# Where the sum of the four weight blocks of chunk 4 is made: by an adding transfer, or by VectorE

## The chip, the core and the metric

The kernel runs on one core of a Trainium2 chip. The metric is the device time of one execution in microseconds (us), as the median of several runs. The changed kernel is timed against the kernel before on the same chip.

The engines are TensorE (PE in the profile, its weight loads PEld), VectorE (DVE), ScalarE (ACT), GpSimd (POOL) and SyncE (SP). Each has its own list of instructions and works through it from the front. SP and POOL issue the transfers (DMA).

## The reference

Two layers of a hybrid model, on 256 tokens of width 1024, in float32. Each layer has two gated nets (`ffn1` and `ffn2`, with 2816 hidden columns), a mixer and a cross attention, each followed by a layer norm.

```python
def swiglu(x, w_gate, w_up, w_down):
    return (jax.nn.silu(x @ w_gate) * (x @ w_up)) @ w_down

for l in range(DEPTH):
    h = layer_norm(ALPHA * h + 0.5 * swiglu(h, ffn1_gate[l], ffn1_up[l], ffn1_down[l]), ...)
    ...  # mixer, cross attention
    h = layer_norm(ALPHA * h + 0.5 * swiglu(h, ffn2_gate[l], ffn2_up[l], ffn2_down[l]), ...)
```

The change lies in the first two products of a net, `x @ w_gate` and `x @ w_up`.

## The kernel before

**A product in three parts.** Each float32 operand is split into a rounded high part (ScalarE, line 75) and the low remainder (VectorE, line 76, which subtracts the high part that ScalarE has just made). TensorE multiplies high by high, high by low and low by high (line 132). So each raw weight tile of 128 x 1024 numbers (512 KB) that comes in costs a transfer, one cast on ScalarE (`whi`) and one subtraction on VectorE (`wlo`).

**A net.** The 2816 hidden columns are worked through in chunks: five of 512 columns and chunk 5 with 256. Between the products of a chunk, TensorE multiplies finished activations of earlier chunks with slabs of the `down` weights (`both`, `slab`; sums in the tiles `dn`). There are four nets. In the last three (`ffn2` of layer 0, `ffn1` and `ffn2` of layer 1) chunks 2, 3, 4 and 5 are made by `by_seven` (line 665).

**Seven products in place of eight.** For a chunk, gate and up weights are cut into an upper and a lower half of rows: `w00` is the gate's upper block, `w01` the up's upper, `w10` the gate's lower and `w11` the up's lower one. A block of a full chunk is two tiles of 128 x 1024. Two token tiles by two halves of x make a product of 2 x 2 by 2 x 2 blocks, and `by_seven` makes it with seven block products, from sums of weight blocks (built in place in `w00` and `w01`) and sums of x blocks (`bx`). The runs of a full chunk, in order:

1. `o` = x00 by `w00` (line 741); `w00 += w01` on VectorE, and `one` = bx0 by that (line 743).
2. `o` += x01 by `w10` (line 746).
3. `w00 += w11` on VectorE; `total` += bx1 by that (line 750). `less` is minus `total` (line 754).
4. `total` += bx2 by `w01` (line 757), which an adding transfer has made the sum of both up blocks.
5. VectorE reads `total` out (`put`, line 758, which runs line 721; it makes the tile `halves`).
6. `less` += bx3 by `w11` (line 759).
7. `total` += x11 by the sum of all four blocks (line 760). This adds to the bank that step 5 reads, so it can't start before step 5 is done.

The sum of all four blocks is made by `more(w00, gate, 1)` (line 752): POOL issues two transfers (line 738) that read the gate's lower block from memory once more and add it to `w00`, after the splits of `w00 + w01 + w11` have read it.

**Where the blocks lie.** The buffers of a chunk rotate (`homes`, lines 688 to 693). In chunk 4 of the three nets `w00` lies in two of the six `raw` buffers, `w01` in `spare0` and `spare1`, `w11` in `lng` and `lnb`, and `w10` in `spare2` and one `raw` buffer. Chunk 5 comes right behind and puts its own `w00` into `spare2`; its other three blocks and the `down` slabs take `raw` buffers. A load into a buffer waits until the last reader of what was there is done, and on SP all that is listed behind it waits with it.

**Order.** The engines' lists are made when the program is built, by a scheduler that looks at dependencies and priorities; a few places are tied by hand (`issue_after`). So an edit in one place can reorder its surroundings.

Of the kernel before, what the change touches and what calls it, by code (L numbers as in the profile page):

```python
# [28 lines left out]
CHUNK = 512  # L29
# [31 lines left out]
def model(ctx: ExitStack, tc: tile.TileContext, t: dict, out: bass.AP):  # L61
# [12 lines left out]
    def split(hi, lo, src):  # L74
        rounded = nc.scalar.copy(hi, src)  # L75
        lows.append(nc.vector.tensor_tensor(lo, src, hi.bitcast(F32), op=ALU.subtract))  # L76
        return rounded
# [78 lines left out]
    def mm_rows(o, xh, xl, wh, wl, start, stop, more=False):  # L156
        product(o, xh, wh, start, False, more)
        product(o, xh, wl, False, False, more)
        product(o, xl, wh, False, stop, more)

    def tok(i):
        return slice(i * P, (i + 1) * P)
# [313 lines left out]
    def ffn(l, name, n, pend=None, last=False, early=None, started=None, following=None):  # L476
        gate, up, down = (t[f"{name}_{x}"][l] for x in ("gate", "up", "down"))
        with tc.tile_pool(name="ffn", bufs=2, reuse_waits="tile") as fp:
# [186 lines left out]
            def by_seven(c0, ncol, bx, between):  # L665
                deep = 1024 // ncol

                def rows_by_columns(r):
                    return r.rearrange("p (k c) -> p k c", c=ncol)

                def pieces(*tags):
                    return [
                        rows_by_columns(
                            (fp if "spare" in g else wp).tile([P, DM], F32, tag=g, name="raw", bufs=6 if g == "raw" else 1)
                        )
                        for g in tags
                    ]
# [5 lines left out]
                def block(m, j, to):  # L683
                    for i, x in enumerate(to):
                        loads.append(nc.sync.dma_start(x, part_of(m, j, i)))
                    return to
# [7 lines left out]
                w00 = block(gate, 0, pieces(*homes[0]))  # L694
                w01 = block(up, 0, pieces(*homes[1]))
                w10 = block(gate, 1, pieces(*homes[3]))

                def parts_of(r, plus=None):
                    hi, lo = [], []
                    for i in range(len(r)):  # L700
                        if plus is not None:
                            nc.vector.tensor_tensor(r[i], r[i], plus[i], op=ALU.add)  # L702
                        h = wp.tile([P, 1024], F32R, tag="whi", name="whi", bufs=8)
                        w = wp.tile([P, 1024], F32R, tag="wlo", name="wlo", bufs=8)
                        h, w = (rows_by_columns(x) for x in (h, w))
                        split(h, w, r[i])
                        hi.append(h)
                        lo.append(w)
                    return Weights(hi, lo, deep, [])

                def part_of_x(i, j):
                    d = slice(4 * j, 4 * j + 4)
                    return xTh[:, d, tok(i)], xTl[:, d, tok(i)]

                def run(o, x, w, more=False):
                    for k in range(4):
                        wh, wl = w.at(k, slice(0, ncol))
                        mm_rows(o, x[0][:, k, :], x[1][:, k, :], wh, wl, k == 0 and not more, k == 3, more)

                def put(o, a, op, b):  # L720
                    nc.vector.tensor_tensor(ordered(o), ordered(a), in_order(b), op=op)  # L721
# [8 lines left out]
                def bank():  # L730
                    return acc((P, CHUNK))[:, 0:ncol]
# [4 lines left out]
                def more(to, m, j):  # L736
                    for i, x in enumerate(to):
                        nc.gpsimd.dma_start(x, part_of(m, j, i), accum_op=ALU.add)  # L738

                o, total, one = (bank() for _ in range(3))  # L740
# [7 lines left out]
                activate(s, 0, o)  # L748
                w11 = block(up, 1, pieces(*homes[2]))
                run(total, bx[1], parts_of(w00, w11), True)  # L750
                if ncol == CHUNK:
                    more(w00, gate, 1)
                less = bank()
                copied = nc.scalar.mul(less, total, -1.0)
# [1 line left out]
                if ncol == CHUNK:  # L756
                    run(total, bx[2], parts_of(w01), True)
                    put(f, e, ALU.subtract, total)
                    run(less, bx[3], parts_of(w11), True)
                    run(total, part_of_x(1, 1), parts_of(w00), True)  # L760
                else:
                    run(less, bx[3], parts_of(w11), True)
                    run(total, bx[2], parts_of(w01), True)
                    put(f, e, ALU.subtract, total)
                    with tc.issue_after(copied.ins):
                        w = parts_of(w00, w10)
                    between[2]()
                    run(total, part_of_x(1, 1), w, True)
# [48 lines left out]
            sevens = (2, 4) if early is not None else (2, 3, 4, 5)  # L817
# [27 lines left out]
            for c, (c0, ncol) in enumerate(chunks):  # L845
                if not c:
                    acts.append(first()())
                    ys = [[acc((P, 512), "dn") for _ in range(2)] for _ in range(NT)]
                elif c in sevens:
                    half = []  # L850

                    def deal_last():
                        acts[4] = acts[4]()

                    left = by_seven(
                        c0, ncol, bx,
                        [lambda: both(*todo.pop(0))] * 2 if ncol == CHUNK else
                        [lambda: (half.append(slab(3, 0)), both(3, 0, half[0], (0,))), deal_last, lambda: both(3, 0, half[0], (1,))],
                    )
                else:  # L860
                    acts.append(hidden(c0)() if ncol == CHUNK else last_hidden(c0, turn_memory))
# [595 lines left out]
```

## Time and profile before

| | us |
|---|---|
| median of three runs (lowest, highest) | 1076.18 (1074.79, 1076.83) |
| the profiled execution | 1078.4 |
| its span, first to last instruction | 1076.5 |
| TensorE busy (matmuls) | 1050.8 (98%) |
| VectorE busy | 956.7 (89%) |
| ScalarE busy | 680.4 (63%) |
| GpSimd busy | 110.0 (10%) |

The trace tells of the profiled execution alone, and every place in it is given in us from the start of its span. Rows of the timeline give the start, the time taken, engine, line, operation, output and inputs, the number of like instructions merged, and in brackets the idle time of the engine before it with what ended it. Operations of helpers all have the helper's line: line 76 is every low part, line 132 nearly every matmul.

### The profile page before, as it was taken

The page shows a single profiled execution, that of the slowest core. Times are in us where ns is not written, and L with a number is a line of the kernel's source. Part 1 is how long each engine was busy: PE and PEld are TensorE (multiplying, and loading weights), DVE is VectorE, ACT ScalarE, POOL GpSimd, SP SyncE. Part 2 cuts the span into 40 slices and gives each one's busy share as a digit, 9 for nine tenths or more (in the row PEclk, how much of TensorE's full clock was granted, in tenths as well). Part 3 has the DMA queues.
Part 4 walks back from the last instruction along what each step waited for, and adds up shares of the span by engine and source line. Part 5 has one row for each costly group of instructions (what it writes and reads, how often), then busy time and mean ns, then how long its engine had stood idle before and what let it go on. Part 6 is the DMA issues. An engine that isn't in the chain of part 4 may idle for free.

```text
span 1076.5 us, 16511 instructions
## 1 busy us (share of the span) xinstructions
PE 1050.8 (98%) x5978; PEld 930.9 (86%) x5978; DVE 956.7 (89%) x1257; ACT 680.4 (63%) x936; POOL 110.0 (10%) x140
## 2 busy tenths in 40 slices
PE   9999999999999999998999998999999999999987
PEld 7888888989899888887888887998998998888876
DVE  6998898989989789998998998899899779889988
ACT  6675775676466557666657566676773657557661
POOL 8001001000000001110001101010000000011101
PEclk9999999999999999999999998999999999999999
DMA  9999985854676589998789999766646665899972
GB/s 364 290 297 296 256 276 158 260 175 122 224 262 208 175 263 269 265 280 251 247 274 278 279 274 258 257 226 226 204 131 217 213 234 172 261 284 275 260 233 69
DMA packets 145569, 257.35 MB, mean 239 GB/s; under 512 B 11440, under 2 KB 52176, under 8 KB 145488
## 3 DMA queue, kind: packets, MB, share of 16 engines
q1 hardware_dynamic: 130656, 228.89, 63.9%
q0 software_dynamic: 14256, 26.23, 14.2%
q10 hardware_dynamic: 576, 1.18, 0.3%
q8 instruction: 47, 0.77, 0.3%
q14 instruction: 34, 0.28, 0.1%
HBM read 240.80 MB, written 1.05 MB: 225 GB/s over the span
## 4 chain that ended last, share of the span: by engine, by line
PE 70%; issue 12%; DMA 8%; DVE 7%; ACT 2%; POOL 1%; DVEq 0%; POOLq 0%; SPq 0%; ACTq 0%
PE acc L132 44%; PE dn L132 23%; DMA raw<-in_ffn_gate_dram 6%; DVE wlo L76 3%; ACT whi L75 2%; DMA raw<-in_ffn_up_dram 2%; DVE raw L702 1%; PE acc L199 1%; POOL raw L738 1%; DVE halves L721 0%; PE dn L1135 0%; DMA raw<-in_ffn_down_dram 0%; DVE h L407 0%; DMA h<-in_x_dram 0%; PE dn L1209 0%
## 5 line engine op out<-in xcount | busy, mean ns | idle before, releaser
L76 DVE TENSOR_TENSOR wlo<-raw,whi 128x1024 fp32r<-128x1024 f32 (+1 forms) x470 | 552.0, 1208 | 47.6 <-ACT whi L75 42.8
L75 ACT CAST whi<-raw 128x1024 fp32r<-128x1024 f32 (+1 forms) x470 | 471.1, 1041 | 187.5 <-DVE raw L702 75.2
L132 PE MATMUL acc<-whi,xT 128*128 128x512 f32 (+1 forms) x944 | 282.2, 376 | 13.8 <-DVE halves L721 13.5
L132 PEld LDWEIGHTS acc<-whi,xT 128*128 128x128 f32 x944 | 178.4, 191 | 39.9 <-issue 13.2
L132 PE MATMUL acc<-wlo,xT 128*128 128x512 f32 (+1 forms) x472 | 176.9, 375 | 0.2 <-DVE wlo L76 0.2
L132 PE MATMUL dn<-whi,ah 128*128 128x512 f32 x346 | 130.3, 381 | 2.2 <-ACT whi L75 2.2
L132 PE MATMUL dn<-wlo,ah 128*128 128x512 f32 x346 | 131.2, 379 | 0.0
L132 PE MATMUL dn<-whi,al 128*128 128x512 f32 x346 | 131.1, 379 | 0.0
L132 PE MATMUL acc<-xT,whi 128*128 128x512 f32 x480 | 117.6, 381 | 0.0
L132 PEld LDWEIGHTS acc<-wlo,xT 128*128 128x128 f32 x472 | 90.5, 192 | 12.6 <-DVE wlo L76 0.6
L132 PEld LDWEIGHTS acc<-xT,whi 128*128 128x128 f32 x480 | 86.8, 190 | 9.8
L132 PE MATMUL dn<-whi,xT 128*128 128x512 f32 x288 | 87.7, 380 | 0.0
L132 PE MATMUL acc<-whi,kTh 128*128 128x512 f32 (+1 forms) x224 | 80.2, 358 | 0.0
L132 PE MATMUL acc<-wlo,kTh 128*128 128x512 f32 (+1 forms) x224 | 79.9, 357 | 0.0
L132 PE MATMUL acc<-whi,kTl 128*128 128x512 f32 (+1 forms) x224 | 79.9, 357 | 0.0
L132 PEld LDWEIGHTS dn<-whi,ah 128*128 128x128 f32 x346 | 65.2, 189 | 12.1 <-ACT whi L75 3.4
L132 PEld LDWEIGHTS dn<-whi,al 128*128 128x128 f32 x346 | 65.4, 189 | 9.2
L132 PEld LDWEIGHTS dn<-wlo,ah 128*128 128x128 f32 x346 | 65.4, 189 | 9.1 <-DVE wlo L76 0.3
L132 PEld LDWEIGHTS acc<-xT,wlo 128*128 128x128 f32 x480 | 62.9, 191 | 3.2
L702 DVE TENSOR_TENSOR raw<-raw 128x1024 f32<-128x1024 f32 x53 | 63.8, 1216 | 0.2
L132 PE MATMUL acc<-xT,wlo 128*128 128x256 f32 x480 | 63.2, 275 | 0.0
L132 PEld LDWEIGHTS dn<-whi,xT 128*128 128x128 f32 x288 | 54.4, 189 | 7.5
(250 smaller groups left out, 1339.5 us busy)
## 6 DMA issues: line engine op xcount, KB each, us to landing
raw<-in_ffn_up_dram SPq DMA_DIRECT2D x88, 512.0 KB, 6.1
raw<-in_ffn_down_dram SPq DMA_DIRECT2D x88, 512.0 KB, 5.9
raw<-in_ffn_gate_dram SPq DMA_DIRECT2D x84, 512.0 KB, 6.0
raw<-in_w_in_dram SPq DMA_DIRECT2D x48, 512.0 KB, 4.7
raw<-in_ffn_up_dram POOLq DMA_DIRECT2D x25, 512.0 KB, 6.3
raw<-in_ffn_gate_dram POOLq DMA_DIRECT2D x22, 512.0 KB, 9.1
dealt<-sg SPq DMA_DIRECT2D x80, 128.0 KB, 4.6
raw<-in_ca_k_dram SPq DMA_DIRECT2D x16, 512.0 KB, 5.1
```

What stands on the lines that cost most here:

```text
L75: rounded = nc.scalar.copy(hi, src)
L76: lows.append(nc.vector.tensor_tensor(lo, src, hi.bitcast(F32), op=ALU.subtract))
L132: turns.append(nc.tensor.matmul(o, w, x, start=start, stop=stop, skip_group_check=more))
L199: turns.append(nc.tensor.transpose(pt[:, k, :], src[:, (4 * j + k) * P : (4 * j + k + 1) * P], unit))
L702: nc.vector.tensor_tensor(r[i], r[i], plus[i], op=ALU.add)
L738: nc.gpsimd.dma_start(x, part_of(m, j, i), accum_op=ALU.add)
```

## The change

In the last three nets, chunk 4 no longer issues `more(w00, gate, 1)`. Its step 7 passes `w10` to `parts_of`, which adds it to `w00` with two VectorE instructions (line 702) just before the splits. `w10` thus has to stay in its two buffers (`spare2` and one `raw`) until these are done. Chunks 2 and 3 of these nets and the first net are as before.

```diff
                 run(total, bx[1], parts_of(w00, w11), True)
-                if ncol == CHUNK:
+                by_transfer = ncol == CHUNK and (len(sevens) < 4 or c0 != 4 * CHUNK)
+                if by_transfer:
                     more(w00, gate, 1)
                 less = bank()
...
                     run(less, bx[3], parts_of(w11), True)
-                    run(total, part_of_x(1, 1), parts_of(w00), True)
+                    run(total, part_of_x(1, 1), parts_of(w00, None if by_transfer else w10), True)
                 else:
```

How the instructions move is shown for the first of the three nets; the other two move alike. First VectorE, at the end of chunk 4 and the start of chunk 5, before. Here `raw_4731` and `raw_4732` are the two tiles of chunk 4's `w00`, `raw_4851` and `raw_4852` those of its `w11`, `acc_4746` is `total`, `acc_4879` is `less`, and `raw_4980`, `raw_4982` and `raw_4984` are `w00`, `w01` and `w10` of chunk 5:

```order
L76 TENSOR_TENSOR wlo_4943<-raw_4852,whi_4942 128x1024
L76 TENSOR_TENSOR wlo_4959<-raw_4731,whi_4958 128x1024
L76 TENSOR_TENSOR wlo_4963<-raw_4732,whi_4962 128x1024
L76 TENSOR_TENSOR wlo_4991<-raw_4980,whi_4990 128x1024
L702 TENSOR_TENSOR raw_4980<-raw_4980,raw_4982 128x1024
L721 TENSOR_TENSOR halves_4744<-halves_4744,acc_4746 128x512
L76 TENSOR_TENSOR wlo_5009<-raw_4980,whi_5008 128x1024
L721 TENSOR_TENSOR halves_4744<-halves_4744,acc_4879 128x512
L76 TENSOR_TENSOR wlo_5027<-raw_4984,whi_5026 128x1024
```

And the same place with the change, where `raw_4739` and `raw_4740` are chunk 4's `w10`:

```order
L76 TENSOR_TENSOR wlo_4941<-raw_4852,whi_4940 128x1024
L702 TENSOR_TENSOR raw_4731<-raw_4731,raw_4739 128x1024
L702 TENSOR_TENSOR raw_4732<-raw_4732,raw_4740 128x1024
L76 TENSOR_TENSOR wlo_4958<-raw_4731,whi_4957 128x1024
L76 TENSOR_TENSOR wlo_4963<-raw_4732,whi_4962 128x1024
L721 TENSOR_TENSOR halves_4744<-halves_4744,acc_4746 128x512
L721 TENSOR_TENSOR halves_4744<-halves_4744,acc_4877 128x512
L76 TENSOR_TENSOR wlo_4991<-raw_4980,whi_4990 128x1024
L702 TENSOR_TENSOR raw_4980<-raw_4980,raw_4982 128x1024
L776 TENSOR_TENSOR sg_4743<-sg_4743,halves_4744 128x1024
L76 TENSOR_TENSOR wlo_5009<-raw_4980,whi_5008 128x1024
L76 TENSOR_TENSOR wlo_5027<-raw_4984,whi_5026 128x1024
```

The two sums of line 702 are new, both reads of chunk 4's results (line 721) stand ahead of chunk 5's first low part and first sum, where before they stood behind them, and the gating product (line 776, line 775 before) has come forward too.

Second SP, from the second tile of a `down` slab in chunk 4 on, before; `raw_4980`, `raw_4982`, `raw_4984` and `raw_5067` are the four blocks of chunk 5, one tile each:

```order
L98 DMA raw_4882<-in_ffn2_down_dram 128x1024
L685 DMA raw_4980<-in_ffn2_gate_dram 128x4x256
L685 DMA raw_4982<-in_ffn2_up_dram 128x4x256
L685 DMA raw_4984<-in_ffn2_gate_dram 128x4x256
L98 DMA raw_5042<-in_ffn2_down_dram 128x1024
L98 DMA raw_5043<-in_ffn2_down_dram 128x1024
L321 DMA lng_5156<-in_ln_g_dram 128x1024
L322 DMA lnb_5157<-in_ln_b_dram 128x1024
L685 DMA raw_5067<-in_ffn2_up_dram 128x4x256
```

And with the change:

```order
L98 DMA raw_4880<-in_ffn2_down_dram 128x1024
L685 DMA raw_4982<-in_ffn2_up_dram 128x4x256
L685 DMA raw_4984<-in_ffn2_gate_dram 128x4x256
L98 DMA raw_5042<-in_ffn2_down_dram 128x1024
L321 DMA lng_5156<-in_ln_g_dram 128x1024
L322 DMA lnb_5157<-in_ln_b_dram 128x1024
L685 DMA raw_4980<-in_ffn2_gate_dram 128x4x256
L98 DMA raw_5043<-in_ffn2_down_dram 128x1024
L685 DMA raw_5067<-in_ffn2_up_dram 128x4x256
```

Chunk 5's first block (`raw_4980`), whose buffer `spare2` now holds `w10` longer, has moved from ahead of its sister blocks to a place behind the two parameter rows of the layer norm.

On POOL the two adding transfers of each of the three nets are gone, six in all. ScalarE has as many instructions as before. TensorE has the same matmuls; between chunk 5's runs and the `down` products some have changed places.

## The prediction

> **What bounds the kernel now.** First the page's span and its row of TensorE, then the chain of waits of TensorE:
>
> ```profile
> span 1076.5 us, 16511 instructions
> PE 1050.8 (98%) x5978; PEld 930.9 (86%) x5978; DVE 956.7 (89%) x1257; ACT 680.4 (63%) x936; POOL 110.0 (10%) x140
> ...
> PE acc L132 <- DVE halves L721: 13.5, 4, 4.5
> ```
>
> TensorE is the bound: it sits idle for 25.7 us in all, and 13.5 of these in four waits for line 721, VectorE's read of a finished bank. The timeline of TensorE shows the three long ones, each in one of the three changed nets, at step 7 of chunk 4:
>
> ```profile
> 490.56 0.38 PE L132 MATMUL acc<-wlo,kTh 128*128 128x512 f32 x1
> 490.77 0.38 PE L132 MATMUL acc<-whi,kTl 128*128 128x512 f32 x1
> 494.71 0.45 PE L132 MATMUL acc<-whi,xT 128*128 128x512 f32 x1 [3.56 <-DVE halves L721]
> ...
> 660.03 0.38 PE L132 MATMUL acc<-whi,kTl 128*128 128x512 f32 x1
> 664.93 0.77 PE L132 MATMUL acc<-whi,xT 128*128 128x512 f32 x1 [4.52 <-DVE halves L721]
> ...
> 1024.91 0.38 PE L132 MATMUL acc<-whi,kTl 128*128 128x512 f32 x1
> 1029.30 0.76 PE L132 MATMUL acc<-whi,xT 128*128 128x512 f32 x1 [4.01 <-DVE halves L721]
> ```
>
> Matmuls follow each other at 0.21 to 0.22 us (490.56 to 490.77). From start to start, less 0.22, the stops cost 3.72, 4.68 and 4.17 us. The view by stretches shows that two of them cost more:
>
> ```profile
> core 0: us, PE busy (x) PEld busy (x) DVE busy (x) ACT busy (x) POOL busy (x), PEclk, DMA share, GB/s
> ...
> 494.70:497.50 2.80, 2.79 (x14) 2.48 (x15) 2.37 (x3) 2.80 (x4) 0.87 (x1) 1.00 0.55 104
> ...
> 664.90:670.20 5.30, 5.27 (x13) 4.21 (x14) 4.85 (x5) 3.26 (x4) 0.87 (x1) 0.50 0.70 100
> ...
> 1029.30:1032.40 3.10, 3.10 (x8) 2.49 (x9) 2.68 (x3) 3.10 (x4) 1.29 (x1) 0.51 0.25 32
> ```
>
> Behind the stops of 4.68 and 4.17 us the granted clock (PEclk) is 0.50 and 0.51, behind that of 3.72 it stays 1.00. Half of 5.3 us and half of 3.1 us are lost besides: 2.65 and 1.5. So this place loses 3.7, 7.3 and 5.7 us. The Trainium skill's page "TensorE: Matmul & The Clock Gate" (Part 1: The HAM clock gate) says that an idle window of about 3.4 us, which runs freely, halves the clock. The trace agrees: the two stops above 4 us did it, the one of 3.72 did not.
>
> What VectorE did meanwhile, in the first of the three nets (its timeline):
>
> ```profile
> 482.70 5.76 DVE L76 TENSOR_TENSOR wlo<-raw,whi 128x1024 fp32r<-128x1024 f32 x5
> 490.35 2.36 DVE L76 TENSOR_TENSOR wlo<-raw,whi 128x1024 fp32r<-128x1024 f32 x2 [1.89 <-ACT whi L75]
> 492.74 1.23 DVE L702 TENSOR_TENSOR raw<-raw 128x1024 f32<-128x1024 f32 x1
> 493.89 0.68 DVE L721 TENSOR_TENSOR halves<-halves,acc 128x512 f32<-128x512 f32 x1
> 495.13 1.22 DVE L76 TENSOR_TENSOR wlo<-raw,whi 128x1024 fp32r<-128x1024 f32 x1 [0.57 <-ACT whi L75]
> ...
> 500.28 1.22 DVE L702 TENSOR_TENSOR raw<-raw 128x1024 f32<-128x1024 f32 x1
> 501.42 1.22 DVE L775 TENSOR_TENSOR sg<-sg,halves 128x1024 f32<-128x1024 f32 x1
> ...
> 508.41 2.36 DVE L76 TENSOR_TENSOR wlo<-raw,whi 128x1024 fp32r<-128x1024 f32 x2 [1.11 <-ACT whi L75]
> ...
> 524.63 0.68 DVE L377 SCALAR_TENSOR_TENSOR h<-h,dn 128x512 f32<-128x512 f32 x1
> ```
>
> And what it waited for at 490.35: POOL's two adding transfers, the least, median and largest time from their issue to landing, and ScalarE's casts.
>
> ```profile
> 477.36 2.42 POOL L738 DMA_DIRECT2D raw<-in_ffn_gate_dram  x2 [10.19 <-DVE wlo L76]
> ...
> DMA to landing us min/median/max: 6.3/8.5/10.8
> ...
> 489.27 2.00 ACT L75 CAST whi<-raw 128x1024 fp32r<-128x1024 f32 x2 [3.05 <-DMA raw<-in_ffn_gate_dram]
> ```
>
> The second adding transfer landed 10.8 us after its issue at 478.5, at 489.3. The cast of its tile ended at 490.3 and the low part at 491.6. Line 721, which TensorE needs, stood behind that, one more low part and a sum: 493.89. Otherwise VectorE hardly rests: from 482.70 to 508.41 its idle time is 1.89, 0.57 and 1.11 us, 3.57 together. The x5 row gives its pace: five in 5.76 us, the last taking 1.22, so 1.14 from start to start.
>
> **The change, part by part**, in the times of the first net.
>
> *Removed:* two adding transfers of 512 KB and the wait for them. Their issue cost POOL alone.
>
> *Added:* two sums of 1.14 us on VectorE. Their inputs have long been there. They take the place of the last of the five low parts, at 487.25 and 488.39, and end at 488.47 and 489.6. The casts follow, each 1.04 long and some 0.1 behind its sum: 489.6 and 490.7. The low parts start at 489.65 and 490.8. Then line 721 comes at once: 491.9 to 492.6, and TensorE goes on 0.14 later, as it did before (494.57, 494.71): at 492.75 in place of 494.71. A stop of 1.75 us stays, too short for the low clock by the rows above.
>
> *Moved:* chunk 5's first block. SP's rows before, and then times to landing:
>
> ```profile
> 472.42 0.43 SPq L685 DMA_DIRECT2D raw<-in_ffn_gate_dram  x1
> ...
> 486.22 0.33 SPq L321 DMA_DIRECT2D lng<-in_ln_g_dram  x1
> 487.36 0.33 SPq L322 DMA_DIRECT2D lnb<-in_ln_b_dram  x1
> 488.49 0.38 SPq L685 DMA_DIRECT2D raw<-in_ffn_up_dram  x1
> ...
> DMA to landing us min/median/max: 5.9/5.9/5.9
> ...
> DMA to landing us min/median/max: 6.2/6.2/6.2
> ...
> DMA to landing us min/median/max: 5.8/5.8/5.8
> ...
> DMA to landing us min/median/max: 5.1/5.1/5.1
> ...
> 661.82 0.33 SPq L98 DMA_DIRECT2D raw<-in_ffn_down_dram  x1
> ...
> DMA to landing us min/median/max: 3.1/3.1/3.1
> ```
>
> The first landing is that of the row at 472.42, the block in question, which so lay there from 478.4 on. With the change its load waits for the first of the two sums and goes out at 488.5, just where the row at 488.49 stood. That row's landing is the second, and its like in the other two nets are the third and fourth: 6.2, 5.8 and 5.1 us, with adding transfers still on the way. The last, 3.1, is that of the row at 661.82, a tile of a `down` slab that went out alone. Queued on SP behind the new wait are another slab tile, which waits for the second sum, and chunk 5's last block: out at about 490.9 in place of 488.49, so landed by 497.1 even at 6.2, and VectorE adds it only at 500.28 or later. How long the moved load takes without the adding transfers no row shows: between 3.1 and 6.2. I take 4.6, the middle: landed at 493.1.
>
> From there a chain that was hidden before: cast 493.2 to 494.25; low part 494.3, for which VectorE has waited since 493.1; sum with `w01` 495.4 to 496.6; cast of it, behind an activation, 496.7 to 497.75; its low part 497.8, against 495.13 before. TensorE has finished step 7 at 495.35 (12 matmuls from 492.75), the first run of chunk 5 at 496.9, and waits for these: 0.2 at 495.4, 1.05 at 496.9, and about 1.05 more for the cast and low part behind it.
>
> On VectorE, up to the row of 508.41: work, plus 2 x 1.14 = 2.28. Idle: 1.2 for the block, 1.2 for the cast of chunk 5's next sum, since the gating product (at 501.42 before) that used to fill this gap now comes earlier, and 1.1 as before at the last sum: 3.5 against 3.57. So that row comes 2.1 to 2.2 us later. From there to the layer norm (524.63, which started without a wait) VectorE has no slack, and TensorE runs within half a us of it (it kept VectorE waiting 0.50 at 525.8):
>
> ```profile
> 525.82 0.69 DVE L377 SCALAR_TENSOR_TENSOR h<-h,dn 128x512 f32<-128x512 f32 x1 [0.50 <-PE dn L132]
> ...
> 511.25 0.35 PE L132 MATMUL acc<-whi,xT 128*128 128x256 f32 x1 [0.35 <-ACT whi L75]
> ```
>
> TensorE so arrives some 0.3 us less late: 1.8 later than before in this net. It had lost 3.7 there, and 0.5 at 511.25. So the same course with the change loses 4.2 + 1.8 = 6.0, now in many small stops.
>
> *The sum.* The other two nets have the same instructions there, so 6.0 each. Before, they lost 7.3 and 5.7. Differences: +1.8, -1.3, +0.3: +0.8 us on the profiled span of 1076.5. The span lies 1.9 below its execution's 1078.4, and the median of the runs is 1076.18; I carry the difference over to the median. Forecast: 1076.18 + 0.8 = 1077.0. About 0.2%, or 2.15 us, is what a measurement of this kernel can tell from no change.
>
> Bounds: each us by which the block lands later than 4.6 costs 1 us in each net: at 6.2, 3 x 1.6 = 4.8 more, 1081.8. Earlier helps little: the sum's cast stands behind the activation of step 7's result (TensorE's end 495.5, activation to 496.2), so at 3.1 only 0.4 per net, 1075.8. The Trainium skill's page "DMA: Bandwidth & Descriptors" (Anatomy of one DMA) fits 2.0 us plus bytes over 436 GB/s to a transfer on GpSimd's path, an estimate of 3.2 us for 512 KB. By it the sum would be 1075.8. The trace doesn't bear it out at this place, where GpSimd's two took 6.3 and 10.8; only the lone slab's 3.1 is as short.
>
> **The rivals.**
>
> *Slower: the moved load is late.* If it takes what its neighbours took, VectorE stands idle from 493.1 to as late as 495.8 and the clean stop of before is paid again in chunk 5. It decides from a landing of about 5.1 us on (0.8 + 3 x 0.45 makes the 2.15 of a measurable loss). For it: all three rows at that place. Against: these had the adding transfers beside them. Price 1081.8; 30%.
>
> *Slower: the low clock.* TensorE's work between 491 and 500 falls into pieces with some 4.5 us of stops. If that halves the clock as in two nets before, another 1.5 to 2.65 us go per net: 1081.5 to 1085.0. Against it: the longest piece is 1.75 us, and 3.72 passed unpunished. 9%.
>
> *Faster: VectorE has room after all.* If the three idle times (3.5 us a net) take up the two sums, so that no work is added in effect, the row of 508.41 comes 2.28 - 3.5 = 1.2 us earlier, and each net gains 2.1 + 1.2 = 3.3 against the forecast: 1077.0 - 9.9 = 1067.1. For it: the stops of before, 17 us in all, are the largest idle time in the kernel, and line 721 does come sooner. Against: the idle times are waits for casts of sums, which more speed elsewhere doesn't shorten. 20%.
>
> That the change doesn't do what it says is ruled out: the lists show six transfers gone and six sums added.
>
> **How the numbers follow.** Forecast 41%, late load 30%, faster 20%, low clock 9%. The forecast's own range is 1075.8 to 1081.8, and one row misread by 0.5 us a net moves it by 1.5. The whole range leaves out the lower half of the faster case and the upper part of the low clock: 1070 to 1083. Faster by over 0.2% (below 1074.0): the rival, and little of the forecast, 0.22. Slower (above 1078.3): both slower rivals, 0.39. Within: 0.39.
>
> **What would show it.** Right: the waits of TensorE for line 721 fall from about 3.6, 4.5 and 4.0 us to under 2 each; the granted clock stays near 1.00 behind them; the load of chunk 5's first block goes out right behind the rows of the layer norm and lands 4 to 5 us later; chunk 5 shows new stops of about 1 us. Wrong: no new stops in chunk 5 (the faster case), a landing of over 5.1 us, or a clock of 0.5 in chunk 5.

## The result, and the profile after

The changed kernel takes 1082.02 us (median of five runs, 1080.45 to 1083.80), the kernel before 1076.83 beside it (five runs, 1074.79 to 1078.40). The ratio is 1.0048, with a 95% interval of 1.0030 to 1.0066: slower by some 5.2 us, in the range of the prediction and above its forecast of 1077.0. Ratios here and below are of fast runs alone: of the six runs of e12, a kernel below, one took 1376.37 us at a granted clock of 0.752, which is left out of its ratio but not of its median of 1070.85 (1070.22 without it).

The profiled execution is the fastest of the five, 1080.45. The page's first lines and TensorE's waits:

```profile
span 1078.7 us, 16498 instructions
PE 1052.4 (98%) x5978; PEld 928.1 (86%) x5978; DVE 963.5 (89%) x1263; ACT 680.6 (63%) x936; POOL 102.7 (10%) x134
...
PE acc L132 <- DVE halves L721: 5.0, 3, 1.7
PE acc L132 <- ACT whi L75: 2.9, 4, 0.8
PE acc L132 <- DVE wlo L76: 2.8, 4, 0.9
PE acc L132 <- ACT acc L742: 2.5, 3, 0.8
```

VectorE has six instructions and 6.8 us more (six sums of 1.14). The waits for line 721 went from 13.5 to 5.0 us, three of at most 1.7. Waits of 0.8 to 0.9 us, of kinds that the kernel before had once each at most, have come in their place. In the first of the three nets TensorE's timeline has them in a row:

```profile
489.98 0.38 PE L132 MATMUL acc<-whi,kTl 128*128 128x512 f32 x1
491.94 0.45 PE L132 MATMUL acc<-whi,xT 128*128 128x512 f32 x1 [1.57 <-DVE halves L721]
...
496.37 0.38 PE L132 MATMUL acc<-wlo,xT 128*128 128x256 f32 x1 [0.88 <-DVE wlo L76]
498.70 0.38 PE L132 MATMUL acc<-whi,kTh 128*128 128x256 f32 x1 [0.84 <-ACT whi L75]
499.92 0.38 PE L132 MATMUL acc<-whi,xT 128*128 128x256 f32 x1 [0.84 <-ACT acc L742]
```

The first row stood at 490.77 before, so this execution comes to the place 0.79 us earlier; times below are often moved by such a shift, to the clock of the kernel before. The second row is step 7, and the matmuls of 256 columns are chunk 5. Row by row, TensorE's lateness against the kernel before grows by 3.4 us over this net (from -0.79 to +2.58 at 530.79), by 0.4 over the second and by 1.7 over the third, 5.4 together. Elsewhere the instructions are the same and the two executions still differ: the kernel before had a stop of 1.56 us at 964 that the changed one hadn't.

VectorE's timeline at the same place, with the sum at 509.03 being the third of chunk 5:

```profile
486.48 2.36 DVE L702 TENSOR_TENSOR raw<-raw 128x1024 f32<-128x1024 f32 x2
488.82 2.37 DVE L76 TENSOR_TENSOR wlo<-raw,whi 128x1024 fp32r<-128x1024 f32 x2
491.11 1.47 DVE L721 TENSOR_TENSOR halves<-halves,acc 128x512 f32<-128x512 f32 x2
495.09 1.23 DVE L76 TENSOR_TENSOR wlo<-raw,whi 128x1024 fp32r<-128x1024 f32 x1 [2.51 <-ACT whi L75]
496.35 1.22 DVE L702 TENSOR_TENSOR raw<-raw 128x1024 f32<-128x1024 f32 x1
497.49 1.22 DVE L776 TENSOR_TENSOR sg<-sg,halves 128x1024 f32<-128x1024 f32 x1
498.68 4.63 DVE L76 TENSOR_TENSOR wlo<-raw,whi 128x1024 fp32r<-128x1024 f32 x4
...
505.62 3.50 DVE L76 TENSOR_TENSOR wlo<-raw,whi 128x1024 fp32r<-128x1024 f32 x3 [1.17 <-ACT whi L75]
509.03 1.22 DVE L702 TENSOR_TENSOR raw<-raw 128x1024 f32<-128x1024 f32 x1
511.36 1.23 DVE L76 TENSOR_TENSOR wlo<-raw,whi 128x1024 fp32r<-128x1024 f32 x1 [1.11 <-ACT whi L75]
```

The largest idle time is 2.51 us, for the cast of chunk 5's first block. ScalarE's row says what that cast waited for, SP's rows when the load went out, and the view by source how long it took in the three nets:

```profile
494.01 1.04 ACT L75 CAST whi<-raw 128x1024 fp32r<-128x1024 f32 x1 [4.08 <-DMA raw<-in_ffn_gate_dram]
...
486.60 0.33 SPq L322 DMA_DIRECT2D lnb<-in_ln_b_dram  x1
487.74 0.38 SPq L685 DMA_DIRECT2D raw<-in_ffn_gate_dram  x1
...
DMA to landing us min/median/max: 6.2/6.2/6.2
...
DMA to landing us min/median/max: 5.5/5.5/5.5
...
DMA to landing us min/median/max: 5.7/5.7/5.7
```

It landed at 493.94. The granted clock (the third number from the end of a row), by stretches of the second net:

```profile
670.00:672.50 2.50, 0.89 (x4) 0.70 (x5) 2.50 (x3) 2.50 (x4) 1.29 (x1) 0.95 0.08 10
672.50:675.00 2.50, 2.50 (x14) 2.50 (x13) 2.50 (x3) 1.61 (x3) 0.00 (x0) 0.50 1.03 165
675.00:677.50 2.50, 2.50 (x16) 2.37 (x16) 1.51 (x2) 1.13 (x3) 0.00 (x0) 0.87 1.23 253
```

Behind chunk 5's cluster of short stops the clock was halved here. In the other two nets it stayed at 1.00.

### The profile page after: what moved, and what is told of

The parts are those of the page before. It is cut to its first block, busy times and chain, and to the rows that moved or that the text cites. A ratio compares the mean times of both kernels' runs of the same rounds, so it can differ in the third digit from the quotient of the medians.

```text
span 1078.7 us, 16498 instructions
## 1 busy us (share of the span) xinstructions
PE 1052.4 (98%) x5978; PEld 928.1 (86%) x5978; DVE 963.5 (89%) x1263; ACT 680.6 (63%) x936; POOL 102.7 (10%) x134
## 3 DMA queue, kind: packets, MB, share of 16 engines
q0 software_dynamic: 12624, 23.09, 12.5%
q10 hardware_dynamic: 576, 1.18, 0.3%
## 4 chain that ended last, share of the span: by engine, by line
PE 80%; DVE 8%; DMA 5%; ACT 4%; issue 3%; POOL 0%; DVEq 0%; ACTq 0%; SPq 0%
PE acc L132 54%; PE dn L132 23%; DVE wlo L76 5%; ACT whi L75 3%; DMA raw<-in_ffn_gate_dram 3%; DVE raw L702 1%; DMA dealt<-both 1%; PE acc L199 1%; DMA raw<-in_ffn_down_dram 1%; DVE square L531 1%; PE dn L1136 0%; DMA h<-in_x_dram 0%; PE dn L1210 0%; DVE al L76 0%; PE acc L581 0%
## 5 line engine op out<-in xcount | busy, mean ns | idle before, releaser
L702 DVE TENSOR_TENSOR raw<-raw 128x1024 f32<-128x1024 f32 x59 | 71.0, 1220 | 0.2
L738 POOL DMA_DIRECT2D raw<-in_ffn_up_dram x25 | 30.3, 1211 | 338.7 <-DMA raw<-in_ffn_down_dram 137.9
```

## The experiments

The first theory (T): the late load of chunk 5's first block is the loss. Its rival R1: the six sums are, by their time on VectorE. All ratios are against the kernel before on the same chip. The last two columns are of the first of the three nets: how much later than before chunk 5's third sum starts on VectorE (shifts at entry taken off), and what TensorE loses over the net. Before, the third sum is this row:

```profile
506.08 1.22 DVE L702 TENSOR_TENSOR raw<-raw 128x1024 f32<-128x1024 f32 x1
```

| kernel | median us | ratio (95%) | third sum | net |
|---|---|---|---|---|
| e3, no sums, load early | 1066.01 | 0.9910 (0.9897–0.9923) | -1.9 | -1.9 |
| e12, half the change, edge | 1070.85 | 0.9930 (0.9905–0.9954) | 0.0 | -0.3 |
| e5, before, edge | 1073.43 | 0.9967 (0.9953–0.9980) | 0.0 | -0.3 |
| e7, change, spare1, edge | 1074.23 | 0.9973 (0.9960–0.9985) | +1.0 | +1.2 |
| e6, change, edge | 1074.58 | 0.9983 (0.9970–0.9996) | +1.0 | +1.2 |
| e11, half the change | 1077.48 | 0.9993 (0.9977–1.0008) | +2.0 | +1.6 |
| e9, before, two edges | 1075.56 | 0.9998 (0.9983–1.0013) | +1.1 | +0.7 |
| e1, change, spare1 | 1078.15 | 1.0016 (1.0003–1.0030) | +2.0 | +1.7 |
| e2, change, sums early | 1078.60 | 1.0023 (1.0008–1.0037) | +1.3 | +1.6 |
| e8, change, rows behind | 1080.40 | 1.0040 (1.0024–1.0056) | +3.0 | +2.7 |
| e4, no sums, load late | 1080.08 | 1.0043 (1.0029–1.0057) | +1.9 | +2.1 |
| the change | 1082.02 | 1.0048 (1.0030–1.0066) | +3.7 | +3.4 |

One more kernel, e10, with both edges of e9 and the first of them at every full chunk, took 1106.51 us. It no longer computes the reference's result, so its time says nothing for or against a theory.

**e1, the load early, the sums kept.**

```diff
-                    homes = [("spare2",), ("raw",), ("raw",), ("raw",)]
+                    homes = [("spare1",), ("raw",), ("raw",), ("raw",)]
```

> The changed kernel with one word changed: in the last three nets, chunk 5's first block lies in spare1, which chunk 4's second block leaves free about 3 us earlier, not in spare2, which the two VectorE sums now hold to 487.7. The sums stay. Theory T (the loss is the late load of chunk 5's first block, landed 5.5 to 6.2 us after an issue that the sums hold back): the load goes out ahead of the layer-norm rows, 2 to 3 us earlier, VectorE's idle 2.51 us ahead of chunk 5's first low part is gone, TensorE's stops in chunk 5 fall from 4.4, 3.5 and 4.2 us to under 2 each, and the time is 1074 to 1078, 4 to 8 below the changed kernel's 1082.0. Rival R1 (the loss is the six sums themselves, 6 x 1.14 = 6.8 us of VectorE time): no change, 1080.5 to 1083.5. Rival R3 (the loss is the queue: whatever is moved, something of the layer-norm rows, the slab and the block is late): also 1080.5 to 1083.5, but with the stops at another place.

VectorE, chunk 5's first low part, first and third sum:

```profile
493.27 1.22 DVE L76 TENSOR_TENSOR wlo<-raw,whi 128x1024 fp32r<-128x1024 f32 x1
...
495.01 1.22 DVE L702 TENSOR_TENSOR raw<-raw 128x1024 f32<-128x1024 f32 x1
497.40 1.23 DVE L76 TENSOR_TENSOR wlo<-raw,whi 128x1024 fp32r<-128x1024 f32 x1 [1.18 <-ACT whi L75]
...
508.88 1.22 DVE L702 TENSOR_TENSOR raw<-raw 128x1024 f32<-128x1024 f32 x1
```

The load went out at 485.90 and landed at 489.58; the 2.51 us before the first low part are gone, and of the 5.2 us some 3.5 came back. T's range ends at 1078, the median is 1078.15: most of the loss goes with the late load, but 1.7 us stay that T has no place for. The edit moved more than the load: the gating product, which filled the wait behind the first sum in the changed kernel (497.49), stands behind the next low part here, and VectorE waits 1.18 us.

**e2, the sums early.** The two sums stand where the transfers were issued.

```diff
+                elif ncol == CHUNK:
+                    for y, z in zip(w00, w10):
+                        nc.vector.tensor_tensor(y, y, z, op=ALU.add)
```

> The changed kernel with its two VectorE sums made right after step 4's parts, where the kernel before issued the adding transfer, and not ahead of step 7's parts. The fourth block's tiles come free some 6 us earlier and chunk 5's first load goes out ahead of the layer-norm rows. The number of sums is the same. Theory T: chunk 5 starts with its block landed, no stop of over 0.3 us in its first rows, 4 us per net less lost there at most; 1072 to 1078. Rival R1 (the sums' VectorE time): VectorE does the same work ahead of step 7, so 1080 to 1083. A miss for both if the sums, put ahead of the parts of steps 5 and 6, make those late: then new stops at chunk 4's steps 5 and 6 of up to 2.3 us each, 1080 to 1086.

The third case of the expectation came, in another form. TensorE's waits and VectorE's row:

```profile
PE dn L132 <- DVE wlo L76: 7.4, 3, 2.5
...
482.82 9.16 DVE L76 TENSOR_TENSOR wlo<-raw,whi 128x1024 fp32r<-128x1024 f32 x8
```

The sums push the low parts of a `down` slab back, and TensorE stops up to 2.5 us for these in each net. The load is early here too (landed by 486.56), and some 2.7 of the 5.2 us came back: 1078.60 lies between the ranges, just above T's 1078 and under R1's 1080.

**e3 and e4, without the sums: load early, load late.** e3 leaves the fourth block's part of the sum out, and e4 all of it but two columns, whose sums hold `w10` as long as the change does. Shown against the changed kernel:

```diff
-  parts_of(w00, None if by_transfer else w10)
+  parts_of(w00)
+  # e4, ahead of it:
+  for y, z in zip(w00, w10) if not by_transfer else ():
+      nc.vector.tensor_tensor(y[:, 0, 0:2], y[:, 0, 0:2], z[:, 0, 0:2], op=ALU.add)
```

> The changed kernel without the two sums, and without the adding transfer: in the last three nets' chunk 4, step 7 multiplies by the sum of three weight blocks, the fourth block's part of it is left out. Nothing holds spare2, so chunk 5's first load goes out as early as in the kernel before. Theory T and rival R1 agree here: step 7's stop falls under 1 us (VectorE is done with w00's low parts 2.3 us earlier than in the changed kernel) and chunk 5 starts on time; the kernel before lost 4.2, 7.3 and 5.7 us at this place, so 1076.8 - 17.2 + 3 x (0.5 to 1.5) = 1061 to 1064, up to 1067. It is the floor against which the next kernel is read.

> As the kernel without the sums, but in their place VectorE adds two columns of the fourth block's tiles to the first's (128x2 in place of 128x1024): the fourth block is held as long as in the changed kernel, while VectorE does 2 x 1.1 us less. All but two columns of the fourth block's part of the sum are left out. It parts the two costs. Theory T (late load): chunk 5's block lands as late as in the changed kernel, its first parts wait for it, and most of the loss stays: 1074 to 1081, at least 8 us above the kernel without sums. Rival R1 (the sums' own time): the loss goes with the sums, 1061 to 1068, within 3 us of the kernel without sums.

VectorE in e3, chunk 5's first sum, and in e4, its first low part and first sum:

```profile
489.84 1.22 DVE L702 TENSOR_TENSOR raw<-raw 128x1024 f32<-128x1024 f32 x1
```

```profile
494.57 1.23 DVE L76 TENSOR_TENSOR wlo<-raw,whi 128x1024 fp32r<-128x1024 f32 x1 [2.56 <-ACT whi L75]
495.83 1.23 DVE L702 TENSOR_TENSOR raw<-raw 128x1024 f32<-128x1024 f32 x1
```

e3 comes out in its range, although step 7's stop stays at 1.8 to 1.9 us and doesn't fall under 1 (line 721 stands behind chunk 5's first sum there); e4 comes out 14 us above it, as T had it. But e1 is 12 us above e3 too, with the load early and only the sums added, which T can't explain. So each of the two alone takes 12 to 14 us of e3's gain, and both together 16. T as the only cause falls, and so does R1.

Neither edit is pure. Of e4's idle time 2.56 us is for the load, but 1.04 is for the cast behind its two short sums; in e1 1.18 is for the cast behind chunk 5's first sum. Up to the row behind the third sum VectorE is idle for 1.68 us in e3, 3.46 in e1, 5.28 in e4 and 4.79 in the changed kernel. With 2.28 us of sums in e1 and in the change, and some 0.2 in e4, that is 4.1, 3.8 and 5.4 us more than in e3; the third sum starts 3.9, 3.8 and 5.7 later. So the costs overlap because work of the one fills idle time of the other: in the changed kernel the second full sum fills the wait that e4 has behind its short ones, and the product fills the wait of e1.

I call what replaces T and R1 S: what counts is when VectorE gets through chunk 5's sums, by work and idle time together. The table's last columns bear it out: over all twelve kernels the net's cost on TensorE follows the third sum to within 0.5 us in the first net. In the second and third nets of the same traces it does so to within 0.7.

**e5, e6, e7: one order edge.** Line 721 for step 5 goes ahead of the low parts of step 7, in the kernel before (e5), the changed one (e6) and e1 (e7). In e6 and e7 the sums stand ahead of line 721.

```diff
-                    put(f, e, ALU.subtract, total)
+                    taken_out = put(f, e, ALU.subtract, total)
                     run(less, bx[3], parts_of(w11), True)
-                    run(total, part_of_x(1, 1), parts_of(w00), True)
+                    with ExitStack() as behind_put:
+                        if len(sevens) == 4 and c0 == 4 * CHUNK:
+                            behind_put.enter_context(tc.issue_after(taken_out.ins))
+                        w = parts_of(w00)
+                    run(total, part_of_x(1, 1), w, True)
```

> The kernel before, with its adding transfer, and one order edge: in the last three nets' chunk 4, VectorE takes the difference for step 7 (L721, 0.68 us) ahead of the low parts of step 7's first block, not behind them and behind chunk 5's first sum. Theory P (the kernel before stopped 3.7 to 4.7 us at this place because VectorE's order put L721 last, behind a cast that waited for the adding transfer, while VectorE stood idle 1.9 us): step 7 starts at its pace, then waits for its low parts, under 1.5 us; the granted clock stays at 1.0; the loss of 17.2 us over three nets falls to 3 to 6, so 1062 to 1066. Rival Q (the adding transfer itself is what was late; it lands at 489.25, and its low parts must follow): the stop only moves from L721 to the low parts and stays 2 to 3 us, clock unaffected or not; 1070 to 1075.

> The changed kernel with the same order edge: the two sums, then L721, then the low parts of step 7's first block. The scheduler then sets the sums two low parts earlier in VectorE's row, and chunk 5's first load ahead of the layer-norm rows. Theory P: step 7's stop falls from 1.74-1.86 us to under 1 us, chunk 5's stops shrink as its load goes out some 1 to 2 us earlier; 3 x (1 + 2) = 9 us less than the changed kernel, 1070 to 1076. Rival R1 (VectorE's work is what is short): the order changes nothing, 1080 to 1083. In any case above the kernel before with the edge, by the 2.3 us of sums per net if VectorE sets the pace there.

> The changed kernel with both: chunk 5's first block in spare1, and L721 ahead of the low parts of step 7's first block. Theories T and P add: the load is out before the sums end, step 7's stop is under 1 us; 1066 to 1072. If the sums' VectorE time counts (R1), it stays 3 to 7 us above the kernel before with the edge alone. If the load of chunk 5 was not the cause (against T), it equals the changed kernel with the edge alone.

VectorE in e5, then TensorE:

```profile
488.73 0.69 DVE L721 TENSOR_TENSOR halves<-halves,acc 128x512 f32<-128x512 f32 x1 [1.27 <-PE acc L132]
...
493.46 1.23 DVE L702 TENSOR_TENSOR raw<-raw 128x1024 f32<-128x1024 f32 x1
...
506.25 1.22 DVE L702 TENSOR_TENSOR raw<-raw 128x1024 f32<-128x1024 f32 x1
```

```profile
495.81 0.38 PE L132 MATMUL acc<-whi,kTh 128*128 128x256 f32 x1 [0.60 <-ACT whi L75]
497.06 0.38 PE L132 MATMUL acc<-whi,xT 128*128 128x256 f32 x1 [0.87 <-ACT whi L75]
```

Step 7's stop is gone in e5, and the time is 3.5 us less, not 11 to 15: P misses. Q's time came, but not at Q's place: the stop didn't move to step 7's low parts. The third sum starts as late as before (506.25, entry shift 0.13), so the stop moved to chunk 5. What was won lies in the second net, 2.5 us, where the low clock is shorter. The third net costs as much as before (0.2 us more), although the low clock is gone there: the second adding transfer took 12.5 us to landing, and VectorE stood idle for it:

```profile
1023.51 1.23 DVE L76 TENSOR_TENSOR wlo<-raw,whi 128x1024 fp32r<-128x1024 f32 x1 [1.89 <-ACT whi L75]
```

A long stop of TensorE was a sign of VectorE's lateness and not its cause. e6 came in P's range. Its step 7 has no stop, and its only stops in chunk 5 of the first net are of 0.84 and 0.87 us. Yet the clock fell behind them, as in its second net:

```profile
495.00:497.50 2.50, 0.84 (x5) 0.65 (x6) 2.48 (x3) 2.50 (x4) 1.29 (x1) 1.00 0.36 116
497.50:500.00 2.50, 2.50 (x15) 2.50 (x14) 2.50 (x3) 1.75 (x3) 0.00 (x0) 0.52 1.06 171
```

e7 missed its own: with the edge the load is early in e6 as well (out at 485.4, landed at 489.1), so `spare1` adds nothing.

**e8, the term itself.** The layer-norm rows go out behind chunk 5's first load.

```diff
-                    gb = ln_params(l, n)
+                    with ExitStack() as behind_load:
+                        if 5 in sevens:
+                            behind_load.enter_context(tc.issue_after(loads[n0].ins))
+                        gb = ln_params(l, n)
```

> The changed kernel with one order edge on SyncE's queue: the two layer-norm rows of the last three nets go out behind chunk 5's first load, not ahead of it. The load still waits for the sums (spare2), so it goes out at about 487.7 as in the changed kernel, but without two transfers of 512 KB just ahead of it. This changes only the time to landing, the term that the prediction set at 4.6 us and that measured 5.5 to 6.2. Theory T: it lands in 3.7 to 4.6 us (the load of the fourth block, without a neighbour ahead, took 3.6), 1 to 2 us sooner, and the first parts of chunk 5 with it; 3 x (1 to 2) us less than the changed kernel's 1082.0, 1076 to 1079.5: the forecast's 1077.0 lies in it. Rival R1 (the sums' VectorE time is the loss) and rival R3 (what is put behind is late in its turn): 1080.5 to 1083.5.

The load's way in e8, and VectorE:

```profile
DMA to landing us min/median/max: 3.8/3.8/3.8
```

```profile
492.49 1.23 DVE L76 TENSOR_TENSOR wlo<-raw,whi 128x1024 fp32r<-128x1024 f32 x1 [0.91 <-ACT whi L75]
...
494.23 1.22 DVE L702 TENSOR_TENSOR raw<-raw 128x1024 f32<-128x1024 f32 x1
496.61 1.23 DVE L76 TENSOR_TENSOR wlo<-raw,whi 128x1024 fp32r<-128x1024 f32 x1 [1.17 <-ACT whi L75]
497.76 1.22 DVE L776 TENSOR_TENSOR sg<-sg,halves 128x1024 f32<-128x1024 f32 x1
```

The load is 2.4 us quicker, and the idle time for it fell from 2.51 to 0.91, as T said. But the edge also moved the gating product (L776) behind the next low part, where it no longer fills the wait for the sum's cast: 1.17 us came back. So the third sum gained only 0.7 us and the time less than its interval: 1080.40 misses T's range, and lies 0.1 us under that of R1 and R3. R3's case is not seen: the rows and the slab tile behind the load took 6.6 to 8.7 us to landing, but no idle time of VectorE up to the third sum is for them. Besides, the clock fell to half behind chunk 5's stops in two nets here.

**e9, the product later.**

```diff
                     def deal_last():
-                        acts[4] = acts[4]()
+                        with tc.issue_after(second_low[0].ins):
+                            acts[4] = acts[4]()
```

> The kernel before with the edge that sets L721 ahead of step 7's low parts, and a second edge: the product of chunk 4's halves (1.22 us of VectorE) goes behind the low part of chunk 5's second product, not ahead of it. With the first edge alone VectorE had no idle time from 488.7 to 501.7 and TensorE waited for it in chunk 5 (stops of 0.66 and 1.03 us in the first of the three nets). Theory V (VectorE's order at the start of chunk 5 sets those stops): the stop of 1.03 goes, three times: 1070 to 1072.5 against 1073.4. Rival W (VectorE is full there, whatever the order): the stop moves to a later row, or the product's deals to the last slabs come 1.2 us later and TensorE waits for these; 1073 to 1076.

The stops of 0.66 and 1.03 us (idle 0.60 and 0.87 by the timeline) were still there, and the third sum came 1.0 later than in e5, for the reason of e8: the product had filled a gap. V falls, W's time came.

**e11 and e12, half the change.** The first tile's sum by transfer, the second's by VectorE; e12 with the edge.

```diff
-                if by_transfer:
-                    more(w00, gate, 1)
+                if ncol == CHUNK:
+                    more(w00, gate, 1, 2 if by_transfer else 1)
...
-  parts_of(w00, None if by_transfer else w10)
+  parts_of(w00, None if by_transfer else [None, w10[1]])
```

> The change for the second of the two tiles alone: the first tile of w00 still gets its part by the adding transfer (which landed at 483.6 in the kernel before, long before it is needed), the second by one VectorE sum (1.14 us) in place of the transfer that landed at 489.25. spare2, the fourth block's first tile, is then free as early as in the kernel before, and chunk 5's first load goes out there, ahead of the layer-norm rows. Theory S, formed after the other runs (what the place costs follows the start of chunk 5's first sum on VectorE, 492.74 in the kernel before and 497.1 on its clock in the changed one; the late load and the two sums each make it late, and the later of the two decides): one sum lies in the 1.9 us in which VectorE stood idle for the transfer, the load is early, chunk 5's first sum starts at 492 to 493.5 and step 7's stop is under 1.8 us; 1072 to 1076, under the changed kernel by 6 to 10. Rival R1 (each sum costs its VectorE time): half of the change's cost, 1078 to 1080.

> The same with the edge that sets L721 ahead of step 7's low parts. Theory S: chunk 5's first sum starts no earlier than with the edge and the transfers alone (493.3), since VectorE was full from 488.7 on there; the sum only fills what was left of its idle time; 1071.5 to 1075, as the kernel before with the edge, 1073.4. If the late transfer of the second tile still cost something with the edge, it is 1 to 2 us less than that.

VectorE in e11, then in e12:

```profile
488.68 1.22 DVE L702 TENSOR_TENSOR raw<-raw 128x1024 f32<-128x1024 f32 x1
491.01 1.23 DVE L76 TENSOR_TENSOR wlo<-raw,whi 128x1024 fp32r<-128x1024 f32 x1 [1.11 <-ACT whi L75]
...
494.49 1.22 DVE L702 TENSOR_TENSOR raw<-raw 128x1024 f32<-128x1024 f32 x1
```

```profile
486.65 1.22 DVE L762 TENSOR_TENSOR raw<-raw 128x1024 f32<-128x1024 f32 x1
487.98 0.69 DVE L721 TENSOR_TENSOR halves<-halves,acc 128x512 f32<-128x512 f32 x1
...
505.50 1.22 DVE L702 TENSOR_TENSOR raw<-raw 128x1024 f32<-128x1024 f32 x1
```

e11 missed both ranges, just above S and just below R1: the scheduler set its sum last, with 1.11 us of idle time for the cast behind it, and chunk 5's first sum starts at 494.2 on the clock of before, not at 492 to 493.5. That is e1's place to 0.1 us, and the net's cost is e1's too (1.6 and 1.7), though e1 has two sums and another buffer: S's rule held where its placing failed. e12 puts the sum and line 721 into VectorE's idle time. It beats both kernels, by 0.7% against before, and is 2.6 us below e5 by the medians (4.0 by the ratios, as the two ran on different chips): more than the 1 to 2 us of its expectation's last sentence, but on that side. The first net costs the same in both. The third costs 1.8 us less in e12, where the 1.89 us that e5 waits for the transfer are gone, and the second 0.9 less: the clock stays at 1.00 in all three nets, and in e5 it fell in the second.

## Why the prediction was right, and where its size was off

*The stop at step 7: right.* Forecast: TensorE goes on at 492.75 and a stop of 1.75 stays. Measured: 491.94, on the clock of before 492.73, and a stop of 1.74 (489.98 to 491.94, less 0.22).

*The load's place and issue: right.* Behind the two rows of the layer norm, at 487.74 (488.53 on the clock of before; forecast 488.5).

*The load's time to landing: this step failed.* "I take 4.6, the middle" was 6.2, 5.5 and 5.7 us, as late as the neighbours' rows of before, although the adding transfers beside them were gone. e8 shows what made it so: without two transfers of 512 KB just ahead it took 3.8, 3.9 and 3.8. By the prediction's own bound (1 us a net for each us beyond 4.6) the three landings cost 1.6, 0.9 and 1.1 more, 3.6 together: 0.8 + 3.6 = 4.4 us, of the 5.2 measured. This is the slower rival (30%), whose price of 1081.8 was nearly the time; it decides from 5.1 us on, and all three lay above. So the time lies in the range because the range was made to hold this rival, and not by the forecast. The price of 1 us per us is not shown by itself: e8 took 2.4, 1.6 and 1.9 us off the landings, but lost part of it to the moved product. And e1, whose load landed early, is 1.7 us slower than the kernel before, where the prediction has 0.4 us faster for an early load; the 1.18 us a net that its order added are more than that.

*VectorE's account: right but for that term.* Forecast idle times 1.2, 1.2 and 1.1 us; measured 2.51, 1.17 and 1.11. The work was 2.28 as said. Idle 4.79 in place of 3.57 and work 2.28 make 3.5; the third sum is 3.7 late. That TensorE arrives some 0.3 less late than VectorE held too: 3.4.

*By net.* Forecast +1.8, -1.3, +0.3; measured +3.4, +0.4, +1.7: each 1.4 to 1.7 too low, and by that bound the landings account for 1.6, 0.9 and 1.1 of it.

*The low clock (9%): happened in one net of three.* The prediction argued that the longest piece was 1.75 us, too short by its rows. That was the longest, and the clock was halved all the same for some 3.5 us of the second net; e6 has it behind stops of 0.87 us at most. So the length of the longest stop was the wrong sign to go by. But VectorE set the pace there: against e1, whose clock stayed at 1.00, the third sum is 1.7 us later in the first net and 1.2 in the second, as the landings of 6.2 and 5.5 would have it, and no loss to the clock shows. So the price of 1.5 to 2.65 per net was too high for this place.

*VectorE has room (20%): no.* Of the 3.57 us of idle time in this stretch the 1.89 for the transfer did go, but 2.51 for the load came in its place, and the rest are waits for casts of VectorE's own sums, which stayed. e12 shows how much room there is for one sum, in the wait for the transfer, if the order lets it in.

What stays open: the last 0.8 us of the 5.2, which is less than the interval leaves open.

## What to carry to other kernels

When one engine follows another closely, cost a change by the work and the idle time of the one that leads, up to the next place where they meet; a long stop of the follower may only be where the lateness shows, and taking it away moves it. A sum on the leading engine costs its own time plus every wait for a cast that it no longer hides, and a buffer that it holds longer costs the load behind it: in such a stretch the two overlap, so test each alone and both together. For a load that moves in a queue, take the landing times of rows with as many transfers just ahead, not a middle value.

## What the runs showed of the hardware

- A load of 512 KB on SP's queue took 3.8 to 3.9 us to landing with none close ahead of it (e8) and 5.5 to 6.2 us as the third of a row issued every 1.14 us (the changed kernel). With adding transfers beside it, the third of such a row took 5.1 to 6.2 us (the kernel before), so the transfers ahead mattered more here than those beside it.
- The granted clock fell without a long stop. In the second net of the changed kernel it went to 0.50 behind 2.5 us in which TensorE was busy for 0.89; in the first net of e6 to 0.52 behind 2.5 us with 0.84 busy, where no stop was over 0.87 us. It does not always fall: the first net of the changed kernel had 0.82 busy in the 2.5 us from 497.5 and kept 1.00. The Trainium skill's page "TensorE: Matmul & The Clock Gate" (A second HAM failure mode: psum-queue depth-cycling) tells of a clock that swings between half and full rate where TensorE idles briefly and often between groups of matmuls, in a kernel that cycles through PSUM banks. The trace agrees that short pauses can do it, with the 0.50 and 0.52 above; whether the banks have a part in it no run here shows.
